# A 3x3 convolution with 2x2 max pooling: one-bank sums, two offset image lanes, and 32 steps of 12 and 20 in a written-out order

## The chip, the cores and the metric

One core of a Trainium2 chip runs the whole program. The metric is the time of one execution on the device in microseconds (us). The kernel before takes 107.98 us (median of 3 runs, 107.88 to 108.08). The engines, as the profile names them: PE (TensorE, the matmuls) with PEld (its weight loads), DVE (VectorE), ACT (ScalarE), POOL (GpSimd) and SP (SyncE, which here only issues transfers).

## The reference

```
x: (16, 64, 64, 64) f32     weight: (128, 64, 3, 3) f32     pool_size = 2
x_pad = pad(x, 1 on each side of h and w)
conv[b, co] = sum over ci, kh, kw of weight[co, ci, kh, kw] * x_pad[b, ci, kh:kh+64, kw:kw+64]
output[b, c, i, j] = max of conv[b, c, 2i:2i+2, 2j:2j+2]          # (16, 128, 32, 32)
```

## The kernel before

**Tiling.** Images go in pairs: the 64 input channels of one image lie on partitions 0 to 63 and those of the other on 64 to 127. Each matmul contracts over 64 partitions, so the two images' matmuls are issued in turn on the two halves of the array, and two run side by side. A *step* is 16 image rows (a quarter of an image) of one pair: 8 output rows, so 8 x 64 = 512 columns, one PSUM bank per image. There are 8 pairs and 32 steps.

**Two kinds of step.** Pooling needs the larger of an upper conv row y0 and a lower one y1. Let r0, r1 be the two rows of x in question and rm, rp the rows above and below; g0, g1, g2 are the kernel's rows. A *product* is three matmuls (kw = 0, 1, 2) for each image, six in all.

- A "k" step has five products. PA (two products: weights D2 = g2 - g1 on r1, G0 on rm) makes one sum; PB (two: D0 = g0 - g1 on r0, G2 on rp) makes another. After the max of both is taken, PR (G1 on the row sum r0 + r1, "ks") is added to it.
- A "w" step has four products on row sums and differences made beforehand: P2 (GM on r1 - r0, "we"), P0 (G0 on "wz"), P3 (G2 on "wy"), P1 (GP on "ws"). ACT copies minus the sum of P2 into a second bank (the seed, SE) before P0 is added to the first and P3 to the second; the max of both is taken, and then P1 is added.

After either, ACT copies the first sum to SBUF (EV/ev), DVE takes the max of the second sum and this copy, in place in PSUM (MX/mx, line 305), PE adds the last product, ACT copies the odd columns to SBUF (OD/od, line 310), DVE takes the max of even columns and these (CM/cm, line 324), and a transfer stores the result. Capitals are k steps, small letters w steps.

**Where the row operations run.** ks and ws run on DVE, wz and wy on POOL, we on DVE for the first five steps and then on POOL (all line 250). A POOL row operation is made to wait for the last DVE row operation before it in the program (`on_gpsimd`, `behind`).

**Loads.** k pairs are loaded by POOL's queue with a cast to bf16 (`kload`, line 95, tile kx), half an image pair at a time; w pairs are loaded as f32 by SP's queue, one step at a time (`wload`, line 100, two tiles wx), each issued by the store of the k step four earlier. The first two chunks of the first k pair come as f32 (kfirst, ksecond) and are cast by DVE and ACT.

**PSUM.** Four accumulators (`acc`) of two banks each, one bank per image; MX, EV, SE work on both images at once (1024 elements), OD and CM on 512.

**Order.** The program's order is written out by hand: HEAD, nine turns of STEADY, TAIL. Each token is one call; every engine runs its own instructions in this order, and waits by semaphores. One turn of STEADY has one k step and one w step, so 16 of each: 16 x 30 + 16 x 24 = 864 matmuls at line 185. Ahead of them lie 8 matmuls on ones and 28 transposes that turn the weight blocks (T*, V*).

Of the kernel before, what the change touches and what calls it, by code (L numbers as in the profile page):

```python
# [11 lines left out]
def kernel(  # L12
# [8 lines left out]

    nc = tc.nc
    FP32 = mybir.dt.float32
# [12 lines left out]
    N = NP * NQ // 2  # L48
    assert N == 16

    const = ctx.enter_context(tc.tile_pool(name="const", bufs=1))
    kx_pool = ctx.enter_context(tc.tile_pool(name="kx_pool", bufs=3))
    row_pool = ctx.enter_context(tc.tile_pool(name="row_pool", bufs=2))
    ev_pool = ctx.enter_context(tc.tile_pool(name="ev_pool", bufs=3))
    od_pool = ctx.enter_context(tc.tile_pool(name="od_pool", bufs=3))
    o_pool = ctx.enter_context(tc.tile_pool(name="o_pool", bufs=4))
# [4 lines left out]
    acc = [psum.tile([128, 2, R, W], FP32, name=f"acc_{i}") for i in range(4)]  # L61
    free = deque(range(4))
    unset = set(range(4))

# [15 lines left out]

# [7 lines left out]
    wx = [const.tile([128, H + 2, W], FP32, name=f"wx_{i}") for i in range(2)]  # L90

    def kload(j, lo, hi):
        if j not in kx:
            kx[j] = kx_pool.tile([128, H, W], BF16, name="kx")
        return nc.gpsimd.dma_start(out=kx[j][:, lo:hi, :], in_=rows_of(2 * j, lo, hi))  # L95

    def wload(i):
        j, q = divmod(i, NQ)
        lo, hi = chunk(q)
        return nc.sync.dma_start(  # L100
            out=wx[j % 2][:, lo + 1 : hi + 1, :], in_=rows_of(2 * j + 1, lo, hi)
        )
# [16 lines left out]


# [13 lines left out]
    def zero(t, h):  # L134
        return nc.tensor.matmul(
            acc[t][:, h], zeros[:, 0:128], zeros, start=True, stop=True, skip_group_check=True
        )

    turned = {}

    def turned_cols(m):
        lo, hi = BLOCKS[m] - 1, BLOCKS[m] + 3
        tp = acc[turned[m]][:, int(m == "G1")].rearrange("p a b -> p (a b)").bitcast(BF16)
        return lo, hi, tp[:, 0 : (hi - lo) * 128]

    def turn(m):
        turned[m] = turned["GM"] if m == "G1" else free.popleft()
        unset.add(turned[m])
        lo, hi, tp = turned_cols(m)
        for j in range(lo, hi):  # L150
            nc.tensor.transpose(  # L151
                tp[:, (j - lo) * 128 : (j - lo + 1) * 128],
                wq[:, j : j + 2, :].rearrange("a b c -> a (b c)"),
                ident,
            )

    def turn_out(m):
        if m != "GM":
            free.append(turned[m])
# [10 lines left out]


    def taps(t, m0, rows, start=False, skip=None, only=None):
        dst = acc[t]
        if start:
            unset.discard(t)
        for kw in (1, 0, 2):
            i0, i1 = 0, R
            if skip == 0:
                i0 = 1
            if skip == R - 1:  # L180
                i1 = R - 1
            o0, o1, c0, c1 = (0, W, 0, W) if kw == 1 else (1, W, 0, W - 1) if kw == 0 else (0, W - 1, 1, W)
            for half in range(2) if only is None else (only,):
                lo = half * CI
                nc.tensor.matmul(  # L185
                    dst[:, half, i0:i1, o0:o1],
                    wt[lo : lo + CI, m0 + kw - half, :],
                    rows(lo, i0, i1, c0, c1),
                    start=start and kw == 1,
                    stop=True,  # L190
                    skip_group_check=True,
                )

    def step1(t, q):
        first = q * R
        return lambda lo, i0, i1, c0, c1: t[lo : lo + CI, first + i0 : first + i1, c0:c1]
# [6 lines left out]
    ta, tb = {}, {}  # L203

    def pa(i):
        j, q = divmod(i, NQ)
        t = ta["k", i] = free.popleft()
        taps(t, D2, step2(kx[j], 2 * q * R + 1), start=True)
        taps(t, G0, step2(kx[j], 2 * q * R - 1), skip=0 if q == 0 else None)

    def pb(i):
        j, q = divmod(i, NQ)
        t = tb["k", i] = free.popleft()
        taps(t, D0, step2(kx[j], 2 * q * R), start=True)
        taps(t, G2, step2(kx[j], 2 * q * R + 2), skip=R - 1 if q == NQ - 1 else None)

    def pr(i):
        taps(tb["k", i], G1, step1(row["ks", i // NQ], i % NQ))

    def p2(i):  # L220
        t = ta["w", i] = free.popleft()
        taps(t, GM, step1(row["we", i // NQ], i % NQ), start=True)

    def p0(i):
        taps(ta["w", i], G0, step1(row["wz", i // NQ], i % NQ))

    def p3(i):
        taps(tb["w", i], G2, step1(row["wy", i // NQ], i % NQ))

    def p1(i, h=None):  # L230
        taps(tb["w", i], GP, step1(row["ws", i // NQ], i % NQ), only=h)

# [3 lines left out]
    def row_out(name, i):  # L236
        j, q = divmod(i, NQ)
        if (name, j) not in row:
            row[name, j] = row_pool.tile([128, HO, W], BF16, name=name)
        return row[name, j][:, q * R : (q + 1) * R, :]  # L240

    def row_in(t, first, pad):
        a = first + pad
        return t[:, a : a + 2 * R - 1 : 2, :]

    def row_op(engine, name, i, a, b, op):
        j, q = divmod(i, NQ)
        t, pad = (kx[j], 0) if name == "ks" else (wx[j % 2], 1)
        f = 2 * R * q
        return engine.tensor_tensor(  # L250
            out=row_out(name, i), in0=row_in(t, f + a, pad), in1=row_in(t, f + b, pad), op=op
        )

    def ks(i):
        inst = on_vector(row_op(nc.vector, "ks", i, 0, 1, ADD))
        if i == 0:
            behind(kload(0, *chunk(2)), inst)
# [4 lines left out]
    def we(i):  # L262
        if i < 5:
            inst = on_vector(row_op(nc.vector, "we", i, 1, 0, SUB))
            if i < 2:
                behind(wload(i + 2), inst)
        else:
            on_gpsimd(row_op(nc.gpsimd, "we", i, 1, 0, SUB))
# [4 lines left out]
    def wy(i):  # L273
        on_gpsimd(row_op(nc.gpsimd, "wy", i, 2, 0, SUB))
        j, q = divmod(i, NQ)
        if i == 0:
            kload(0, *chunk(3))
        if q == 1 and j + 1 < NP // 2:
            kload(j + 1, 0, H // 2 + 1)
        if q == 2 and j + 1 < NP // 2:  # L280
            kload(j + 1, H // 2 + 1, H)

# [3 lines left out]
    def halves(h):  # L286
        return slice(0, 2) if h is None else slice(h, h + 1)

    def evac(g, h=None):
        if g not in ev:  # L290
            ev[g] = ev_pool.tile([128, 2, R, W], FP32, name="ev")
        nc.scalar.copy(out=ev[g][:, halves(h)], in_=acc[ta[g]][:, halves(h)])  # L292
        done(g, "ev", ta, h)

    def seed(i):
        t = tb["w", i] = free.popleft()
        if t in unset:
            unset.discard(t)
            for h in range(2):
                zero(t, h)  # L300
        nc.scalar.mul(acc[t], acc[ta["w", i]], -1.0)  # L301

    def rowmax(g, h=None):
        t = acc[tb[g]][:, halves(h)]
        nc.vector.tensor_tensor(out=t, in0=t, in1=ev[g][:, halves(h)], op=MAX)  # L305

    def odd(g, h=None):
        if g not in od:
            od[g] = od_pool.tile([128, 2, R, WO], FP32, name="od")
        nc.scalar.copy(out=od[g][:, halves(h)], in_=acc[tb[g]][:, halves(h), :, 1::2])  # L310

    part = {}

    def done(g, what, tiles, h):
        part[g, what] = part.get((g, what), 0) + (2 if h is None else 1)
        if part[g, what] == 2:
            free.append(tiles.pop(g))

    def colmax(g, h=None):
        if g not in ot:  # L320
            ot[g] = o_pool.tile([128, 2, R, WO], FP32, name="o")
        s = halves(h)
        o = ot[g][:, s]
        nc.vector.tensor_tensor(  # L324
            out=o, in0=acc[tb[g]][:, s, :, 0::2], in1=od[g][:, s], op=MAX
        )
        done(g, "cm", tb, h)
        j, q = divmod(g[1], NQ)
        p = 4 * j + 2 * (g[0] == "w")
        dst = out[p : p + 2, :, q * R : (q + 1) * R, :].rearrange("b c h w -> c b (h w)")  # L330
        src = o.rearrange("p b h w -> p b (h w)")
        store = nc.scalar if h == 0 else nc.sync
        store.dma_start(out=dst[:, s], in_=src)  # L333
        if g[0] == "k" and g[1] + NQ < N and h is None:
            wload(g[1] + NQ)


    def cast_rows(first):
        inst = on_vector(
# [6 lines left out]
    def cast_more(first):  # L346
        nc.scalar.copy(out=kx[0][:, klo2 + first : khi2 : 2, :], in_=ksecond[:, first::2, :])

# [12 lines left out]
        "GP": lambda: on_vector(  # L361
            nc.vector.tensor_add(out=slots(GP), in0=gsum, in1=g1)
        ),
# [4 lines left out]
        "PA": pa, "PB": pb, "PR": pr, "P0": p0, "P1": p1, "P2": p2, "P3": p3,  # L368
        "KS": ks, "WS": ws, "E": we, "Z": wz, "Y": wy, "SE": seed,
# [85 lines left out]
```

## Time and profile before

| quantity | before |
|---|---|
| median of 3 runs | 107.98 us |
| span of the profiled execution (first to last instruction) | 106.2 us |
| mean granted PE clock | 0.982 |
| first / last matmul of line 185 starts | 5.96 / 100.5 us |
| DVE idle before line 305, waiting for PE | 11.4 us in 14 waits |
| ACT idle before line 310 / 292, waiting for PE | 11.5 us / 11.0 us |
| POOL idle before wz, waiting for DVE's ws | 24.3 us in 13 waits |
| HBM read / written | 17.07 MB / 8.39 MB |

The profile is of one execution; the span leaves out what lies around the first and last instruction. In a group of instructions "mean ns" is what one instruction's row lasts; two that follow each other may overlap, so the distance from start to start can be shorter. An issue's "us to landing" goes from the issuing instruction to the end of the last packet.

### The profile page before, as it was taken

The page shows a single profiled execution, that of the slowest core. Times are in us where ns is not written, and L with a number is a line of the kernel's source. Part 1 is how long each engine was busy: PE and PEld are TensorE (multiplying, and loading weights), DVE is VectorE, ACT ScalarE, POOL GpSimd, SP SyncE. Part 2 cuts the span into 40 slices and gives each one's busy share as a digit, 9 for nine tenths or more (in the row PEclk, how much of TensorE's full clock was granted, in tenths as well). Part 3 has the DMA queues.
Part 4 walks back from the last instruction along what each step waited for, and adds up shares of the span by engine and source line. Part 5 has one row for each costly group of instructions (what it writes and reads, how often), then busy time and mean ns, then how long its engine had stood idle before and what let it go on. Part 6 is the DMA issues. An engine that isn't in the chain of part 4 may idle for free.

```text
span 106.2 us, 2337 instructions
## 1 busy us (share of the span) xinstructions
PE 98.7 (93%) x900; PEld 51.2 (48%) x900; DVE 82.3 (78%) x115; ACT 72.3 (68%) x92; POOL 60.6 (57%) x70
## 2 busy tenths in 40 slices
PE   7879999999999999999999999999999999999800
PEld 2444445555555555555555555555555555455300
DVE  1598989889797868696977868687879688668940
ACT  4628976776867677777677676767877776775620
POOL 6208691915439494949385694949293947653000
PEclk9999999999999999999999999999999999999975
DMA  2987999999968589999968399999966503232071
GB/s 53 370 269 269 228 152 314 264 304 304 316 245 211 190 177 187 219 298 195 337 253 208 124 210 202 265 257 213 385 188 167 195 4 122 78 107 96 0 247 49
DMA packets 12619, 21.96 MB, mean 207 GB/s; under 512 B 960, under 2 KB 9280, under 8 KB 12608
## 3 DMA queue, kind: packets, MB, share of 16 engines
q1 hardware_dynamic: 11312, 18.03, 52.9%
q0 software_dynamic: 1152, 3.65, 20.1%
q8 instruction: 7, 0.11, 0.4%
q10 hardware_dynamic: 144, 0.13, 0.4%
q14 instruction: 4, 0.03, 0.2%
HBM read 17.07 MB, written 8.39 MB: 240 GB/s over the span
## 4 chain that ended last, share of the span: by engine, by line
PE 84%; DVE 6%; DMA 4%; ACT 1%; issue 1%; SPq 0%; ACTq 0%; DVEq 0%
PE acc L185 83%; DVE acc L305 5%; DMA kfirst<-in_x_dram 4%; PE acc L151 1%; DVE o L324 1%; ACT od L310 1%; DVE kx L340 0%; SPq L105 0%; ACTq L333 0%; DVEq L305 0%
## 5 line engine op out<-in xcount | busy, mean ns | idle before, releaser
L185 PEld LDWEIGHTS <-wt 64*128 64x128 bf16 x864 | 48.6, 94 | 45.1 <-issue 1.8
L305 DVE TENSOR_TENSOR acc<-acc,ev 128x1024 f32<-128x1024 f32 (+1 forms) x34 | 39.5, 1166 | 11.9 <-PE acc L185 11.4
L185 PE MATMUL acc<-kx,wt 64*128 64x504 bf16 (+3 forms) x384 | 46.6, 373 | 0.6 <-DVE kx L340 0.6
L292 ACT COPY ev<-acc 128x1024 f32<-128x1024 f32 (+1 forms) x34 | 32.6, 964 | 12.5 <-PE acc L185 11.0
L250 POOL TENSOR_TENSOR wz<-wx 128x512 bf16<-128x512 f32 x16 | 20.3, 1271 | 30.3 <-DVE ws L250 24.3
L310 ACT COPY od<-acc 128x512 f32<-128x512 f32 (+1 forms) x33 | 19.0, 574 | 12.5 <-PE acc L185 11.5
L324 DVE TENSOR_TENSOR o<-acc,od 128x512 f32<-128x512 f32 (+1 forms) x33 | 22.1, 674 | 4.5 <-ACT od L310 4.4
L250 POOL TENSOR_TENSOR wy<-wx 128x512 bf16<-128x512 f32 x16 | 20.3, 1270 | 0.0
L301 ACT ACTIVATE acc<-acc 128x1024 f32<-128x1024 f32 x16 | 16.1, 1008 | 1.0 <-PE acc L185 0.5
L250 POOL TENSOR_TENSOR we<-wx 128x512 bf16<-128x512 f32 x11 | 14.1, 1278 | 0.1
L185 PE MATMUL acc<-ws,wt 64*128 64x504 bf16 (+1 forms) x96 | 13.3, 377 | 0.4 <-DVE acc L305 0.4
L185 PE MATMUL acc<-ks,wt 64*128 64x504 bf16 (+1 forms) x96 | 13.3, 377 | 0.1
L185 PE MATMUL acc<-we,wt 64*128 64x504 bf16 (+1 forms) x96 | 13.3, 377 | 0.0
L185 PE MATMUL acc<-wz,wt 64*128 64x504 bf16 (+1 forms) x96 | 13.2, 377 | 0.0
L185 PE MATMUL acc<-wy,wt 64*128 64x504 bf16 (+1 forms) x96 | 13.2, 377 | 0.0
L250 DVE TENSOR_TENSOR ws<-wx 128x512 bf16<-128x512 f32 x16 | 10.9, 684 | 0.0
L250 DVE TENSOR_TENSOR ks<-kx 128x512 bf16<-128x512 bf16 x16 | 6.7, 417 | 0.0
L95 POOL DMA_DIRECT2D kx<-in_x_dram x8 | 4.7, 589 | 2.6 <-DVE ks L250 2.6
L403 PE MATMUL acc<-const-bfloat16-1.0 128*128 128x512 bf16 x8 | 3.2, 572 | 0.8 <-PEq L436 0.8
L250 DVE TENSOR_TENSOR we<-wx 128x512 bf16<-128x512 f32 x5 | 3.6, 722 | 0.1
L354 DVE TENSOR_TENSOR wq<-wraw 128x192 bf16<-128x192 f32 x1 | 0.5, 500 | 2.6 <-DMA wraw<-in_weight_dram 2.6
L151 PE MATMUL acc<-ident,wq 128*128 128x128 bf16 x28 | 2.1, 220 | 0.4 <-DVE wq L354 0.4
(26 smaller groups left out, 15.9 us busy)
## 6 DMA issues: line engine op xcount, KB each, us to landing
out_dram<-o SPq DMA_DIRECT2D x31, 256.0 KB, 3.8
wx<-in_x_dram SPq DMA_DIRECT2D x8, 512.0 KB, 6.8
wx<-in_x_dram SPq DMA_DIRECT2D x4, 544.0 KB, 6.0
wx<-in_x_dram SPq DMA_DIRECT2D x4, 480.0 KB, 4.8
kx<-in_x_dram POOLq DMA_DIRECT2D x3, 528.0 KB, 8.3
kx<-in_x_dram POOLq DMA_DIRECT2D x3, 496.0 KB, 8.7
kfirst<-in_x_dram SPq DMA_DIRECT2D x1, 544.0 KB, 4.3
ksecond<-in_x_dram SPq DMA_DIRECT2D x1, 512.0 KB, 4.9
```

The source lines that it names most:

```text
L95: return nc.gpsimd.dma_start(out=kx[j][:, lo:hi, :], in_=rows_of(2 * j, lo, hi))
L151: nc.tensor.transpose(tp[:, (j - lo) * 128 : (j - lo + 1) * 128], wq[:, j : j + 2, :].rearrange("a b c -> a (b c)"), ident,)
L185: nc.tensor.matmul(dst[:, half, i0:i1, o0:o1], wt[lo : lo + CI, m0 + kw - half, :], rows(lo, i0, i1, c0, c1), start=start and kw == 1, sto ...
L250: return engine.tensor_tensor(out=row_out(name, i), in0=row_in(t, f + a, pad), in1=row_in(t, f + b, pad), op=op)
L292: nc.scalar.copy(out=ev[g][:, halves(h)], in_=acc[ta[g]][:, halves(h)])
L301: nc.scalar.mul(acc[t], acc[ta["w", i]], -1.0)
L305: nc.vector.tensor_tensor(out=t, in0=t, in1=ev[g][:, halves(h)], op=MAX)
L310: nc.scalar.copy(out=od[g][:, halves(h)], in_=acc[tb[g]][:, halves(h), :, 1::2])
L324: nc.vector.tensor_tensor(out=o, in0=acc[tb[g]][:, s, :, 0::2], in1=od[g][:, s], op=MAX)
L354: on_vector(nc.vector.tensor_sub(out=slots(D2), in0=g2, in1=g1))
L403: warm = nc.tensor.matmul(acc[n // 2][:, n % 2], ones[:, 0:128], ones, start=True, stop=True, skip_group_check=True)
```

## The change

- PSUM is held as four one-bank accumulators for each of two lanes; a lane is one image of a pair. EV, MX, SE, OD and CM are done for each lane by itself: 512 elements (256 for OD and CM) instead of 1024 (512).
- The two lanes no longer go in step: a token `a+b` of the order issues the three matmuls of a product of lane 0 in turn with the three of a product of lane 1, and these may belong to different steps and products.
- 12 steps are k and 20 are w (16 and 16 before): three k pairs, five w pairs, in the sequence SEQ. So 12 x 30 + 20 x 24 = 840 matmuls. A third wx tile is added; `we` runs on DVE for 13 steps (token E) and on POOL for 7 (token e).
- Loads: the k loads have tokens of their own in the order, L0 to L5, on POOL's queue between its row operations (`kload_next`); L0 and L1 load steps 2 and 3, L2 to L5 two steps each (4-5, 6-7, 8-9, 10-11). A w load is issued behind the store of a step up to 14 places ahead of its use (LEAD), so the first store is followed by the loads of w steps 4 to 8.
- Stores: one for both lanes on SP's queue; one per lane for the last two steps.
- The order is one list of 140 products and the other engines' calls, without a repeated part.

```
+    SEQ = "KWKWKWKWWKWWKWWKWWKWWKWWKWWKWWKW"
...
-    row_pool = ctx.enter_context(tc.tile_pool(name="row_pool", bufs=2))
-    ev_pool = ctx.enter_context(tc.tile_pool(name="ev_pool", bufs=3))
-    od_pool = ctx.enter_context(tc.tile_pool(name="od_pool", bufs=3))
-    o_pool = ctx.enter_context(tc.tile_pool(name="o_pool", bufs=4))
+    row_pool = ctx.enter_context(tc.tile_pool(name="row_pool", bufs=7))
+    ev_pool = ctx.enter_context(tc.tile_pool(name="ev_pool", bufs=6))
+    od_pool = ctx.enter_context(tc.tile_pool(name="od_pool", bufs=6))
+    o_pool = ctx.enter_context(tc.tile_pool(name="o_pool", bufs=6))
...
-    acc = [psum.tile([128, 2, R, W], FP32, name=f"acc_{i}") for i in range(4)]
-    free = deque(range(4))
+    acc = [
+        [psum.tile([128, R, W], FP32, name=f"acc_{h}_{i}") for i in range(4)] for h in range(2)
+    ]
+    free = [deque(range(4)) for _ in range(2)]
...
+    wx = [const.tile([128, H + 2, W], FP32, name=f"wx_{i}") for i in range(3)]
...
+    def kload(i, n=1):
+        p, q = place["k", i]
+        lo = chunk(q)[0] if i % NQ else 0
+        hi = chunk(q + n - 1)[1]
+        nc.gpsimd.dma_start(out=ktile(i)[:, lo:hi, :], in_=rows_of(p, lo, hi))
...
+    def taps(dst, h, m0, rows, start=False, skip=None):
+        lo = h * CI
+        i0, i1 = int(skip == 0), R - int(skip == R - 1)
+        made = []
         for kw in (1, 0, 2):
...
+            made.append(
+                lambda kw=kw, o0=o0, o1=o1, c0=c0, c1=c1: nc.tensor.matmul(
+                    dst[:, i0:i1, o0:o1],
+                    wt[lo : lo + CI, m0 + kw - h, :],
+                    rows(lo, i0, i1, c0, c1),
...
+    def evac(*g):
+        ev[g] = ev_pool.tile([128, R, W], FP32, name="ev")
+        nc.scalar.copy(out=ev[g], in_=acc[g[2]][ta[g]])
+        free[g[2]].append(ta.pop(g))
+
+    def seed(i, h):
+        t = tb["w", i, h] = take(h, seeded=True)
+        nc.scalar.mul(acc[h][t], acc[h][ta["w", i, h]], -1.0)
+
+    def rowmax(*g):
+        t = acc[g[2]][tb[g]]
+        nc.vector.tensor_tensor(out=t, in0=t, in1=ev.pop(g), op=MAX)
+
+    def odd(*g):
+        od[g] = od_pool.tile([128, R, WO], FP32, name="od")
+        nc.scalar.copy(out=od[g], in_=acc[g[2]][tb[g]][:, :, 1::2])
+
+    LEAD = 14
+    held = deque(range(4, NW))
...
+        if n >= len(order_of) - 2:
+            nc.sync.dma_start(out=dst[:, h], in_=src[:, h])
+        elif stored[c, i] == 2:
+            nc.sync.dma_start(out=dst, in_=src)
+            while held and order_of.index(("w", held[0])) <= n + LEAD:
+                wload(held.popleft())
...
+    def kload_next(n):
+        if n < 2:
+            kload(n + 2)
+        else:
+            i = 2 * n
+            kload(i, min(2, NK - i))
...
+    for s in ORDER.split():
+        if s[0] == "P":
+            made = [product(n, int(i), int(h)) for n, i, h in (p.split(".") for p in s.split("+"))]
+            for matmuls in zip(*made):
+                for matmul in matmuls:
+                    matmul()
```

Some stretches of the new order (an index is the step, then the lane; S is ws):

```
g1 D0 D2 g2 TD0 GS g0 TD2 VD0 TG2 VD2 TG0 TG1 XO VG0 XE PAa.0.0+PAa.0.1 VG2 KS.0 L0 PAb.0.0+PAb.0.1
...
S.2 od.0.0 EV.1.1 P2.1.0+P2.2.1 Z.2 cm.0.0 od.0.1 MX.1.1 PBb.1.0+PBa.2.1 SE.1.0 cm.0.1 Y.2
...
CM.1.0 P1.1.0+P2.1.1 Y.4 CM.2.0 mx.2.1 PAa.3.0+PAb.3.1 SE.2.0 od.1.0 P0.2.0+PBa.3.1 L2 KS.3 EV.3.1
...
P0.3.0+P1.1.1 SE.3.1 CM.3.1 E.6 PR.3.0+P0.3.1 ev.3.0 KS.4 od.1.1 P3.3.0+P2.4.1 Z.5 od.2.0 cm.1.1
OD.3.0 cm.2.0 P2.4.0+P3.3.1 ev.3.1 mx.3.0 SE.4.1 Y.6 PAa.4.0+PAa.4.1 CM.3.0 mx.3.1 P1.3.0+PAb.4.1
...
CM.7.1 CM.7.0 Y.14 SE.12.1 P2.11.0+P0.11.1 mx.12.0 od.9.0 PAa.8.0+P0.12.1 cm.9.0 ev.11.1 L5 S.15
...
P1.11.0+P2.13.1 Z.15 ev.13.0 mx.14.1 P3.13.0+PAa.10.1 od.11.0 SE.13.1 e.15 cm.11.0 P2.14.0+P1.14.1
```

The order ends in:

```
P1.19.0+PR.11.1 mx.19.1 od.18.1 od.17.0 cm.18.1 PR.11.0+P1.19.1 OD.11.1 cm.17.0 od.19.0 CM.11.1
od.19.1 cm.19.0 OD.11.0 cm.19.1 CM.11.0
```

## The prediction

> **What bounds the kernel now.** I read the page's busy times first, then the chain of waits, then the groups by shape, then DVE's timeline, and last the transfers.
>
> ```profile
> span 106.2 us, 2337 instructions
> PE 98.7 (93%) x900; PEld 51.2 (48%) x900; DVE 82.3 (78%) x115; ACT 72.3 (68%) x92; POOL 60.6 (57%) x70
> ...
> 5.96 1.39 PE acc L185 x12
> ...
> 9.64 81.42 PE acc L185 x756
> ...
> 100.07 0.85 PE acc L185 x6
> ```
>
> The third to fifth lines are pieces of the chain (start, length, what). 756 matmuls follow each other for 81.42 us: 0.2154 us per pair, 0.646 us per product, and no other engine in between. PE bounds it. Its account: start 5.96, 432 pairs x 0.2154 = 93.05, 12 transposes after the start x 0.069 (8 take 0.55 in the chain) = 0.83, so 99.84; the last matmul ends at 100.9, so about 1.06 is lost in stalls. From there to the end of the span 5.3 us: od, cm, a store's issue on ACT's queue, od and cm of the other image, and 3.2 us from the last cm's end (103.0) on.
>
> DVE has 22% to spare, and its idle time is mostly waiting for PE. Its rows by shape, and a stretch of its timeline (start, length):
>
> ```profile
> L305 DVE TENSOR_TENSOR acc<-acc,ev 128x1024 f32<-128x1024 f32 x30 | 36.8, 1228 | 11.7 <-PE acc L185 11.4 <-ACT ev L292 0.2
> L324 DVE TENSOR_TENSOR o<-acc,od 128x512 f32<-128x512 f32 x31 | 21.2, 690 | 3.5 <-ACT od L310 3.5
> L305 DVE TENSOR_TENSOR acc<-acc,ev 128x512 f32<-128x512 f32 x4 | 2.7, 696 | 0.2
> L324 DVE TENSOR_TENSOR o<-acc,od 128x256 f32<-128x256 f32 x2 | 0.8, 424 | 1.0 <-ACT od L310 0.8
> ...
> 22.82 0.69 DVE L324 TENSOR_TENSOR o<-acc,od 128x512 f32<-128x512 f32 x1
> 23.42 0.68 DVE L250 TENSOR_TENSOR we<-wx 128x512 bf16<-128x512 f32 x1
> 24.02 0.42 DVE L250 TENSOR_TENSOR ks<-kx 128x512 bf16<-128x512 bf16 x1
> 24.36 0.68 DVE L250 TENSOR_TENSOR ws<-wx 128x512 bf16<-128x512 f32 x1
> ```
>
> A row of 0.69 is followed after 0.60: back to back, an instruction costs about 0.085 less than its row.
>
> **Change 1, fewer matmuls.** 840 instead of 864: 12 pairs x 0.2154 = 2.59 us less, on the bounding engine. Against it: in before, the products at an image's upper and lower edge leave out one of eight rows in both images at once (64 of 512 columns, 3 x 64 columns a product; by the pair's 0.2154 for 512 columns 0.08 us), 8 times, 0.64 us, which the mean 0.2154 holds. In the new order only two of six such products (step 0 and step 7) stand beside their twin; elsewhere the partner has full length. About 0.46 us goes back. The rest of the pairing I cost at nothing: in before too the two matmuls of a pair have different weights, rows and banks.
>
> **Change 2, head and tail.** PAa.0 still needs kfirst and its cast, so the start stays at 5.96; 8 transposes come after it instead of 12: 0.55. Behind the last product there are now OD, CM of 256 elements: 1.27 us (od 0.41, then OD 0.26 later, then CM 0.42, hand-overs 0.04 each) instead of 2.1 with a store's issue in between, then the same 3.2: 4.4 instead of 5.3.
>
> Without stalls: 5.96 + 90.47 + 0.46 + 0.55 + 4.4 = 101.8 us of span. The old span is reached at 4.4 us of stalls; so the stalls decide.
>
> **Change 3, DVE and ACT in half-size pieces.** DVE back to back: MX 64 x 0.61 = 39.0; CM 64 x 0.34 (0.424 - 0.085) = 21.8; ks 12 x 0.335 = 4.0; ws 20 and we 13 x 0.605 = 20.0; weights and casts at the head 4.4; together 89 us, against 91 us of PE work. MX's 0.61 is one of three gaps between 512-element MX in the tail (starts at 97.18, 97.91, 98.52, 99.31: 0.73, 0.61, 0.79). Bounds: 0.61 and their mean 0.71, 6.4 us more over 64; I take 0.61, the gap of every row that waits for nothing, and keep the other. In a sentence of its own: the Trainium skill (Perfetto Trace Analysis, Optimizing Scalar/DVE Operations) gives DVE about 125 ns of overhead on PSUM and 60 on SBUF and advises larger operations where the engine is saturated; here CM, which reads PSUM, shows 0.605 - 512/0.96 GHz = 0.07 us, and by the page's figure an estimate of DVE's sum would be 6 us more.
>
> ACT back to back: the two 512-element ev of step 15 take 1.07 together, so 0.48 each; EV and SE 104 x 0.48, OD 64 x 0.26, head 4: 71 us. POOL: 47 row operations x 1.225 (start to start), six issues x 0.58, head 3: 64 us. Neither bounds.
>
> By place: of DVE's 89 us, 40.7 stand ahead of the 60th of 140 products. DVE starts at 3.7 (weights landed), so done at 44.4 at best; PE gets there at 6.5 (start and transposes) + 59 x 0.646 = 44.6. DVE is full for the first 60 products; between products 34 and 59 it has 16.9 us to do in 16.2. I charge 0.8 us of stall (0.7 of excess, 0.1 of hand-overs); up to 2.6 if MX costs 0.71 (26 of them ahead of the 60th product).
>
> **Change 4, the k loads at their new places.** These rows (all of before's kx loads have 7.5 to 8.8 us) stand against it:
>
> ```profile
> kx<-in_x_dram POOLq DMA_DIRECT2D x3, 528.0 KB, 8.3
> kx<-in_x_dram POOLq DMA_DIRECT2D x3, 496.0 KB, 8.7
> wx<-in_x_dram SPq DMA_DIRECT2D x1, 544.0 KB, 9.5
> ```
>
> The third is the w load issued at 14.6. Before, the k loads had some 15 us: steps 0 to 3 hold 108 pairs, so step 4 begins at about 30.5, and its load was issued at 15.7 (its own row: 8.6).
>
> *L2* (steps 4, 5) stands behind Z.2, Y.2, e.3, Z.3, Y.4 on POOL, and Z.2 behind S.2 on DVE. wload(2) follows E.0 (8.7) and lands 7.0 later (its row in before), so E.2 runs from 15.7, S.2 is done at 16.9; five operations of 1.225 bring L2 to 23.1, and 8.6 more to 31.7. KS.4 needs it, and on DVE cm.1.1, cm.2.0 and mx.3.0 are queued behind KS.4; mx.3.0 must be done for product 38 (P1.3.0) at 6.5 + 37 x 0.646 = 30.4. KS.4 and the three take 1.7, so KS.4 is due at 28.7: **3.0 us late**, on DVE and PE alike. Bounds: 2.0 if PE is already a microsecond late there; 5.8 if Y.4 waits for its rows (wload(4) behind the first store at 15.1, landing 9.5 later, 24.6), which the five w loads in a row could do.
>
> *L5* (steps 10, 11) stands behind Z.14, e.13, Y.14, these behind KS.7, this behind MX.7.0, which waits for product 81 (6.5 + 81 x 0.646 = 58.8, and 0.2 for its last matmul's end). MX 0.61, KS 0.42, three POOL operations 3.7: L5 at 63.9; with the 7.5 to 7.8 of the rows from 60 us on it lands at 71.6. PAa.10.1 is product 99, due at 69.8: **1.7 us late** (1.6 to 2.9 by the longest row). L0, L1, L3, L4 have 7.5 to 16 us and cost nothing; L0 (5.6 to 13.1 for product 11 at 13.0) is even.
>
> In a sentence of its own: the Trainium skill (DMA: Bandwidth & Descriptors, Anatomy of one DMA) gives a load by this path 2.0 us plus its bytes at 436 GB/s, for these 1.08 MB read an estimate of 4.5 us, by which both loads would be in time; the rows here show 7.5 to 8.8 and do not bear it out.
>
> **Sum.** 101.8 + 0.8 + 3.0 + 1.7 = 107.3 us of span. The profiled execution's span of 106.2 lies 1.8 under the median of its runs (107.98); with the same 1.8: **109.1 us**, 1.1 slower than before.
>
> **Rivals.**
> - *The loads land in time*, because POOL reaches them earlier or a load takes the 4.4 to 4.9 us of the quietest rows (wx at 2.7, ksecond at 4.2). For it: the DMA engines' share is 0.71 in the stretch from 30 to 40 us, against 0.96 to 1.04 from 10 to 30. Against it: eight rows of 7.5 and more, at 60 us too. Stalls 0.8 plus some 0.3: 101.8 + 1.1 + 1.8 = **104.7**, faster. It decides from where both loads together are less than 3.6 late instead of 4.7, about half a microsecond each: near. The Trainium skill's DMA page, named above, speaks for this one.
> - *DVE loses its overlap*: with 64 MX and 64 CM each waiting for a result just made, each costs its row and starts after the former one's end: 64 x 0.696 + 64 x 0.424 + ks 5.0 + ws 13.7 + we 9.4 + head 4.6 = 104.3; from 3.7, with 0.5 idle and 3.2 at the end 111.7, so **113.5**. Half of it, 103.9 of span from DVE alone, is under what the loads give, so it decides from six tenths on. Against it: in before, an MX, with PE's sum and ACT's copy to wait for, still started 0.61 after the CM ahead of it (59.45 to 60.06).
> - *The five w loads in a row* hold Y.4 back: L2's upper bound, 2.8 more, **111.9**.
> - *Pairs of unlike products don't run side by side*: then each such product takes twice 0.646, some 60 us more; nothing in the rows speaks for it.
>
> **How the numbers follow.** Forecast 0.52, loads in time 0.26, DVE without overlap 0.14, w loads 0.07, unpaired 0.01. The likeliest gives 109.1, its own range is 106.6 to 111.5 (L2 2.0 to 5.0, L5 1.0 to 2.9, DVE 0.4 to 1.6), which reaches under 107.8: of its 0.52, 0.06 is faster and 0.05 the same. A measurement of this kernel tells some 0.2% (0.2 us) from no change. Faster: 0.26 + 0.06 + 0.01 of the DVE case = 0.33; same 0.06; slower 0.61. The range for 8 in 10 reaches to the loads in time below and the w loads above: 104.6 to 112.2.
>
> **What would show it.** PE's rows with a gap of 1.5 us or more ahead of product 38 and of product 99, the releaser DVE's mx behind KS.4, and the kx load; DVE idle at KS.4 until a transfer; six kx issues of 7.5 us or more; MX of 512 elements 0.61 apart where DVE is full; line 185 with 840 matmuls at 0.108 each between stalls; 4.4 us from the last matmul to the end. It is wrong if PE runs through 23 to 35 us and 60 to 75 us without a gap: then a load took under 6 us or POOL came to it earlier, and the time is under 106.

## The result and the profile after

| quantity | before | after |
|---|---|---|
| median of the runs | 108.03 us (run again beside it) | 116.38 us (114.80, 116.10, 116.66, 119.89) |
| ratio to before, with 95% interval | | 1.0675 [1.0578, 1.0773]: slower |
| profiled execution, span | 106.2 us | 114.80 us, 113.0 us |
| mean granted PE clock | 0.982 | 0.975 |
| first matmul of the products starts | 5.96 us | 6.03 us |
| end of the last matmul to end of span | 5.3 us | 5.3 us |

The ratios here and below leave disturbed executions out, so that a ratio can lie below the quotient of the medians, and none is given where too few are left.

The page of after, its first lines, the granted clock in 40 slices of 2.8 us, and the groups that answer to DVE's lines shown of before:

```profile
span 113.0 us, 2473 instructions
PE 100.8 (89%) x877; PEld 53.1 (47%) x877; DVE 93.1 (82%) x184; ACT 81.4 (72%) x177; POOL 64.6 (57%) x74
...
PEclk9999999999998599999999999999999999999995
...
L300 DVE TENSOR_TENSOR acc<-acc,ev 128x512 f32<-128x512 f32 x64 | 42.3, 691 | 4.1 <-PE acc L211 2.4
...
L315 DVE TENSOR_TENSOR o<-acc,od 128x256 f32<-128x256 f32 x64 | 24.9, 416 | 3.2 <-ACT od L304 2.5
...
kx<-in_x_dram POOLq DMA_DIRECT2D x2, 528.0 KB, 9.1
kx<-in_x_dram POOLq DMA_DIRECT2D x2, 496.0 KB, 8.3
```

PE is busy in 89% of the span instead of 93%, and no other engine is full. The slices 13 and 14 have a low clock; before had no such place ahead of its last matmul. DVE's rows have the sizes that were forecast (0.69 and 0.42 us), and the two-step k loads take 7.8 to 9.4 us (each of the two lines gives the middle of two loads).

The chain of waits, whole where PE runs and broken where it does not (start, length, what):

```profile
35.73 32.71 PE acc L211 x280
...
72.25 7.81 DMA kx<-in_x_dram
...
80.11 25.37 PE acc L211 x232
```

The stretch around the larger break, in the timeline of all engines (start, length; in brackets the idle time before and what ended it):

```profile
34.59 0.42 DVE L260 TENSOR_TENSOR ks<-kx 128x512 bf16<-128x512 bf16 x1 [3.46 <-DMA kx<-in_x_dram]
...
34.93 0.75 DVE L315 TENSOR_TENSOR o<-acc,od 128x256 f32<-128x256 f32 x2
...
35.60 0.69 DVE L300 TENSOR_TENSOR acc<-acc,ev 128x512 f32<-128x512 f32 x1
35.73 1.46 PE L211 MATMUL acc<-kx,wt 64*128 64x512 bf16 x6 [3.06 <-DVE o L315]
...
36.97 0.63 PE L211 MATMUL acc<-ws,wt 64*128 64x512 bf16 x1
```

KS.4 stands still for 3.46 us until L2 has landed; behind it on DVE come the two cm and mx.3.0, and PE is idle for 3.06 us. It goes on with product 37 (products are counted from 1, as in the prediction), as soon as the second cm has freed a bank; the prediction had named product 38 and mx.3.0. What was not forecast is in the last line: a matmul now lasts 0.63 us instead of 0.38. The table by stretches has the clock (columns: stretch, its length, busy us and instructions of PE, PEld, DVE, ACT, POOL, then granted clock, DMA share, GB/s):

```profile
34.00:36.00 2.00, 0.27 (x2) 0.22 (x4) 1.41 (x4) 0.56 (x1) 0.91 (x1) 0.92 0.29 112
36.00:38.00 2.00, 2.00 (x12) 0.90 (x10) 2.00 (x4) 0.61 (x2) 2.00 (x3) 0.50 0.93 281
38.00:40.00 2.00, 2.00 (x17) 1.29 (x14) 1.76 (x4) 1.35 (x4) 0.68 (x2) 0.73 0.95 190
```

From 35.7 to 39.1 us the granted clock is 0.50; 3.41 us at half speed cost a full PE 1.7 us. The wait is thus paid for half again after it is over. The four executions of after lie in the order of their mean granted clock: 0.975 with 114.80 us, 0.968 with 116.10, 0.963 with 116.66, 0.945 with 119.89. An estimate from these means (the missing share of the clock, times two, times the span) puts 5.7, 7.3, 8.5 and 13.0 us at half speed. The other three spans are 1.3, 1.9 and 5.1 us longer than the profiled one, and by the estimate lost clock makes up 0.8, 1.4 and 3.7 us of that. At which places they lost it, no trace shows.

The account of after's span, by the starts of its 840 matmuls (839 distances, 0.1077 each without a stall):

| term | us | forecast |
|---|---|---|
| first matmul starts | 6.03 | 5.96 |
| 839 x 0.1077, and the last matmul's row of 0.38 | 90.74 | 90.47 |
| losses up to 20 us (head) | 2.85 | 0.55 |
| gap ahead of product 37 (L2) | 3.42 | 3.0 |
| half clock behind it | 1.7 | not in the sum |
| gap ahead of product 99 (L5) | 1.81 | 1.7 |
| all other losses (edges, DVE) | 1.2 | 1.26 |
| last matmul's end to the end | 5.30 | 4.4 |
| span | 113.0 | 107.3 |

The row "other" is what is left of 10.96 us of losses in all. The 1.7 is worked out from the clock (half of 3.41 us). Before has 1.61 us of losses, about 1.1 of them up to 20 us.

### The profile page after: what moved, and what is told of

Same layout as the page of the kernel before. It is cut to its first block, busy times and chain, and to the rows that moved or that the text cites. A ratio compares the mean times of both kernels' runs of the same rounds, so it can differ in the third digit from the quotient of the medians.

```text
span 113.0 us, 2473 instructions
## 1 busy us (share of the span) xinstructions
PE 100.8 (89%) x877; PEld 53.1 (47%) x877; DVE 93.1 (82%) x184; ACT 81.4 (72%) x177; POOL 64.6 (57%) x74
## 4 chain that ended last, share of the span: by engine, by line
PE 51%; DMA 7%; POOL 3%; DVE 3%; issue 1%; DVEq 0%; POOLq 0%
PE acc L211 51%; DMA kx<-in_x_dram 7%; DVE o L315 2%; POOL wz L260 1%; POOL we L260 1%; POOL wy L260 1%; DVE acc L300 1%; DVEq L483 0%; POOLq L260 0%; DVEq L300 0%
## 5 line engine op out<-in xcount | busy, mean ns | idle before, releaser
L300 DVE TENSOR_TENSOR acc<-acc,ev 128x512 f32<-128x512 f32 x64 | 42.3, 691 | 4.1 <-PE acc L211 2.4
L291 ACT COPY ev<-acc 128x512 f32<-128x512 f32 x64 | 36.0, 593 | 6.3 <-PE acc L211 5.5
L211 PE MATMUL acc<-ws,wt 64*128 64x504 bf16 (+1 forms) x120 | 31.6, 383 | 0.0
L211 PE MATMUL acc<-wy,wt 64*128 64x504 bf16 (+1 forms) x120 | 30.7, 377 | 0.0
L296 ACT ACTIVATE acc<-acc 128x512 f32<-128x512 f32 x40 | 23.1, 585 | 9.7 <-DVE o L315 4.9
L211 PE MATMUL acc<-wz,wt 64*128 64x504 bf16 (+1 forms) x120 | 29.4, 385 | 0.0
L211 PE MATMUL acc<-we,wt 64*128 64x504 bf16 (+1 forms) x120 | 28.3, 377 | 0.2 <-DVE we L260 0.2
L315 DVE TENSOR_TENSOR o<-acc,od 128x256 f32<-128x256 f32 x64 | 24.9, 416 | 3.2 <-ACT od L304 2.5
L304 ACT COPY od<-acc 128x256 f32<-128x256 f32 x64 | 22.3, 379 | 6.2 <-PE acc L211 5.7
L211 PE MATMUL acc<-ks,wt 64*128 64x504 bf16 (+1 forms) x72 | 16.9, 377 | 0.0
L260 DVE TENSOR_TENSOR we<-wx 128x512 bf16<-128x512 f32 x13 | 8.8, 682 | 0.3 <-DMA wx<-in_x_dram 0.3
```

What stands on the lines that cost most here:

```text
L211: lambda kw=kw, o0=o0, o1=o1, c0=c0, c1=c1: nc.tensor.matmul(dst[:, i0:i1, o0:o1], wt[lo : lo + CI, m0 + kw - h, :], rows(lo, i0, i1, c0, c1),
L260: return engine.tensor_tensor(out=r, in0=t[:, f + a : f + a + 2 * R - 1 : 2, :], in1=t[:, f + b : f + b + 2 * R - 1 : 2, :], op=op,)
L291: nc.scalar.copy(out=ev[g], in_=acc[g[2]][ta[g]])
L296: nc.scalar.mul(acc[h][t], acc[h][ta["w", i, h]], -1.0)
L300: nc.vector.tensor_tensor(out=t, in0=t, in1=ev.pop(g), op=MAX)
L304: nc.scalar.copy(out=od[g], in_=acc[g[2]][tb[g]][:, :, 1::2])
```

## The experiments

Two theories stood at the start. **The gaps**: the time is lost where two k loads come too late, and in what PE does after such a gap. **Half-size DVE work** (a rival): DVE cannot keep up in 64 + 64 small pieces, and then moving the loads brings nothing. A third, *the five w loads in a row*, blames the transfers that compete with L2.

**Loads earlier.** e1 moves L2, e2 moves L5, e3 both; nothing else changes.

L2, in e1 and e3:

```
-        P0.0.0+P0.0.1 OD.0.1 S.1 P3.0.0+P3.0.1 Z.1 CM.0.1 ev.0.1 ev.0.0 mx.0.1 PAa.2.0+PAa.2.1 OD.0.0 Y.1
+        P0.0.0+P0.0.1 OD.0.1 S.1 P3.0.0+P3.0.1 Z.1 CM.0.1 ev.0.1 ev.0.0 mx.0.1 PAa.2.0+PAa.2.1 OD.0.0 Y.1 L2
...
-        CM.1.0 P1.1.0+P2.1.1 Y.4 CM.2.0 mx.2.1 PAa.3.0+PAb.3.1 SE.2.0 od.1.0 P0.2.0+PBa.3.1 L2 KS.3 EV.3.1
+        CM.1.0 P1.1.0+P2.1.1 Y.4 CM.2.0 mx.2.1 PAa.3.0+PAb.3.1 SE.2.0 od.1.0 P0.2.0+PBa.3.1 KS.3 EV.3.1
```

L5, in e2 and e3:

```
-        SE.9.1 e.14 P0.10.0+P1.8.1 MX.6.1 P3.10.0+P0.9.1 od.8.1 MX.6.0 ev.10.0 Y.12 P1.8.0+PR.6.1 ev.9.1
+        SE.9.1 e.14 P0.10.0+P1.8.1 MX.6.1 P3.10.0+P0.9.1 od.8.1 MX.6.0 ev.10.0 Y.12 L5 P1.8.0+PR.6.1 ev.9.1
...
-        CM.7.1 CM.7.0 Y.14 SE.12.1 P2.11.0+P0.11.1 mx.12.0 od.9.0 PAa.8.0+P0.12.1 cm.9.0 ev.11.1 L5 S.15
+        CM.7.1 CM.7.0 Y.14 SE.12.1 P2.11.0+P0.11.1 mx.12.0 od.9.0 PAa.8.0+P0.12.1 cm.9.0 ev.11.1 S.15
```

> Only L2, the load of k steps 4 and 5, is moved ahead: from behind Y.4 to behind Y.1 on POOL's queue, so it is issued at about 17.3 us instead of 25.1. Theory 'late loads': it lands by about 26 us, KS.4 no longer waits, the 3.4 us gap of PE at 32 to 36 us goes, and with it the 1.7 us that the half clock behind it costs: span 113.0 - 5.0 = about 108.0, time about 109.8; the gap at product 99 stays. Rival 'DVE is full': the wait was only where DVE's backlog showed, and PE loses 2 us or more of the 5.0 again in smaller stalls between 30 and 70 us: span 110 or more.

> Only L5, the load of k steps 10 and 11, is moved ahead: from behind Y.14 to behind Y.12 on POOL's queue, issued some 11 us earlier. Theory 'late loads': the 1.8 us gap of PE ahead of product 99 goes, the gap at 32 to 36 us and the half clock stay: span about 111.2, time about 113. Rival 'DVE is full': less than 1 us.

> Both loads, L2 and L5, are moved ahead as in the two runs with one. Theory 'late loads': the gains add, 5.0 + 1.8: span about 106.2, time about 108.0, which is before's. Rival 'DVE is full': under half of it, span 109.5 or more.

| kernel | median us | ratio to before [95%] | span | losses |
|---|---|---|---|---|
| e1 | 111.28 | 1.0161 [1.0080, 1.0241] | 110.0 | 7.12 |
| e2 | 113.73 | none given | 112.4 | 9.82 |
| e3 | 109.58 | 1.0107 [1.0065, 1.0148] | 107.7 | 4.78 |

In e1, L2 is issued at 17.48 instead of 25.14 and lands sooner too (in the microsecond of its issue the share of the transfers on SP's queue is 34% of the DMA engines' time, in after 101%); the page's clock line has no low slice left:

```profile
PEclk9999999999999999999999999999999999999997
```

L2's row in its transfer view:

```profile
kx<-in_x_dram POOLq DMA_DIRECT2D x1, 528.0 KB, 6.3
```

That time varies: 6.3 to 8.8 us in the five kernels with L2 at this place (e1, e3, e5, e6, e7), 9.1 to 10.2 in the five with L2 at after's place (after, e2, e4, e10, e11). The 3.4 us gap is gone and the half clock with it. In its place a loss of 0.89 at 29 us has come: Y.4 now waits for step 4's w rows, whose load runs beside the earlier L2. The gap ahead of product 99 stays (1.91). In e2 it is the other way round: product 99 runs through, and the gap of 4.18 at 36 us and its half clock stay in the profiled execution. (The fastest of e2's four executions, 111.49 us, has a mean clock of 0.993, which leaves 1.5 us at half speed: less than one piece of 3.41, so that there the half clock did not come.) e3 has neither gap. So both loads are causes, each at its own place, and together with the half clock they make up most of the slowdown (1.0675 to 1.0107). The rival falls for this part, but e3 is still slower than before, by 1%.

**The half clock apart from the wait.** e4 lets PE run 13 matmuls on zeros, into a bank that the next product clears, where it would stand idle; e10 is the same with L5 early (to be compared with e2).

```
+        if s == "PAa.4.0+PAa.4.1":
+            for _ in range(13):
+                nc.tensor.matmul(
+                    acc[1][free[1][0]], zeros[:, 0:128], zeros, start=True, stop=True,
+                    skip_group_check=True,
+                )
```

> The loads stay where the change has them. 13 matmuls on zeros are put ahead of product 37, into the free bank that this product clears and fills next, so PE is busy through most of the wait for KS.4. Theory 'the idle gap brings the half clock': the wait stays at 3 to 3.5 us of line 211's matmuls, but the granted clock stays 1.0 between 35 and 40 us, and 1.7 us come back: span about 111.3. Rival 'the half clock is not from the gap': span 113.0 and the clock falls all the same.

> L5 early, and 13 matmuls on zeros ahead of product 37 as in the run that filled the gap. To be compared with L5 early alone (113.7), where the clock fell behind the gap at 32 to 36 us. Theory 'an idle gap of 3 us brings the half clock': with the gap filled and the second gap gone the clock stays full to the end of the matmuls: about 112.0. Rival 'the half clock comes anyway, once in a run': it falls somewhere else, and the time stays at 113 to 114.

e4: 115.79 us, 1.0645 [1.0587, 1.0702], not told apart from after. Its stretches say why (columns as before):

```profile
36.00:38.00 2.00, 1.85 (x19) 0.73 (x17) 2.00 (x5) 1.42 (x3) 1.92 (x3) 1.00 1.10 308
...
77.00:80.00 3.00, 0.70 (x7) 0.21 (x6) 0.88 (x2) 0.90 (x3) 2.18 (x2) 1.00 0.62 196
80.00:84.00 4.00, 4.00 (x24) 1.52 (x22) 2.05 (x4) 1.74 (x5) 2.00 (x2) 0.57 0.02 6
```

The wait for L2 is as long as ever (3.39), but the clock behind it is 1.00, so that it is idleness and not the late load that halves the clock. PE then comes to product 99 1.2 us earlier; L5 is issued earlier by as much (71.05), but takes 8.5 us instead of 7.8, PE idles 2.30 us there instead of 1.64, and now the half clock falls behind this gap, from 80.1 to 83.5 us, for a loss of 1.71. In e10, which has no second gap, the trace shows the gain: the clock is full to the last matmul while the wait for L2 is still 3.20, and the span is 110.4 beside e2's 112.4. Of these 2.0 us the half clock is 1.7. The rest nearly cancels: e10 starts 0.8 earlier and waits 1.0 less for L2, and loses 1.0 more in the head and 0.5 elsewhere. The times, 112.11 us, 1.0329 [1.0277, 1.0380], against e2's median of 113.73, don't show it by themselves, since e2's one execution without the half clock (111.49) is level with e10's.

**The same place, smaller loads.** e8 leaves L2 and L5 where they are and loads one step at a time.

```
-            kload(i, min(2, NK - i))
+            if n in (2, 5):
+                kload(i)
+                kload(i + 1)
+            else:
+                kload(i, 2)
```

> On the changed kernel as it was, the loads stay at their places, but L2 and L5 each become two loads, one step each, in a row. Theory 'a k load is late by its size': the first half lands after some 6 us (the one-step loads of the head took 4.9 to 7.1) instead of 9.4 and 7.8, so the wait for KS.4 falls from 3.4 to under 1, the one ahead of product 99 to under 0.5; time 116.4 - 4 or more, if the half clock goes with the gap: about 111 to 112. Rival 'a k load has a fixed latency of 8 us whatever its size': no change, 115 to 116.

111.47 us, 1.0287 [1.0214, 1.0361], span 109.5. The first halves, in the two transfer views:

```profile
kx<-in_x_dram POOLq DMA_DIRECT2D x1, 272.0 KB, 7.9
...
kx<-in_x_dram POOLq DMA_DIRECT2D x1, 256.0 KB, 6.9
```

Half the bytes land only 1.5 and 0.9 us sooner (9.4 and 7.8 in after): beside the other queues a transfer's time is mostly not its own bytes. The gaps fall by about as much, 3.42 to 1.97 and 1.81 to 0.89 (not to under 1 and 0.5, as was expected), and the PE idle time of 1.61 brings no half clock; so 2.4 us of gap and 1.7 us of half clock are saved, and the ratio falls by 4 points. In the profiled execution the head, too, loses 1.0 less than in after.

**The five w loads.** e11 shortens the lead of the w loads, so that fewer compete with L2.

```
-    LEAD = 14
+    LEAD = 10
```

> LEAD 10 instead of 14, nothing else: the first store is followed by two w loads and not by five. Rival of the prediction 'the five w loads hold the k load back': L2 lands some 1 us or more earlier than after 9.4, the wait for KS.4 falls by as much. Theory 'L2 is late by its place and its size': L2 still takes 8.3 or more, the gap stays over 2.5 us, the time within 1 us of the changed kernel's 115 to 116.

124.18 us, 1.1464 [1.1418, 1.1510]. L2 still takes 9.8 us (issued 25.57), with a gap of 3.87, so the five in a row are not the cause. Competition as such is not ruled out: here too two w loads are issued just ahead of L2 (24.83 and 25.36). And the later w loads are now late; the waits show where (total us, times, longest):

```profile
POOL we L260 <- DMA wx<-in_x_dram: 13.2, 2, 8.9
```

PE loses 6.09 us at 74 us, released by E.12 on DVE, whose ws ahead of it had waited 4.3 us for w rows too, and 2.97 at 90. Idle times of 3.51, 5.85 and 2.81 us were each followed by the half clock, for 3.41, 6.83 and 3.41 us.

**What is left in e3: DVE beside POOL.** In e3 E.4 and Y.4, a row operation on DVE and one on POOL, overlap, and the DVE one lasts 1.75 us:

```profile
25.21 1.45 POOL L260 TENSOR_TENSOR wy<-wx 128x512 bf16<-128x512 f32 x1 [1.80 <-DMA wx<-in_x_dram]
25.45 1.75 DVE L260 TENSOR_TENSOR we<-wx 128x512 bf16<-128x512 f32 x1
...
28.19 0.39 PE L211 MATMUL acc<-we,wt 64*128 64x512 bf16 x1 [0.70 <-DVE o L315]
```

e7 is e3 with Y.4 behind E.4. e5 is e3 with two edits at the head: ksecond issued without waiting for D2, and Y.0 behind Z.0, so that GP on DVE has no POOL operation beside it.

Against e3, e7:

```
-        CM.1.0 P1.1.0+P2.1.1 Y.4 CM.2.0 mx.2.1 PAa.3.0+PAb.3.1 SE.2.0 od.1.0 P0.2.0+PBa.3.1 KS.3 EV.3.1
-        S.3 PAb.3.0+PBb.3.1 ev.2.0 E.4 P3.2.0+P1.2.1 SE.1.1 Y.3 MX.3.1 PBa.3.0+P0.1.1 od.2.1 cm.1.0 mx.2.0
+        CM.1.0 P1.1.0+P2.1.1 CM.2.0 mx.2.1 PAa.3.0+PAb.3.1 SE.2.0 od.1.0 P0.2.0+PBa.3.1 KS.3 EV.3.1
+        S.3 PAb.3.0+PBb.3.1 ev.2.0 E.4 Y.4 P3.2.0+P1.2.1 SE.1.1 Y.3 MX.3.1 PBa.3.0+P0.1.1 od.2.1 cm.1.0 mx.2.0
```

Against e3, e5:

```
-        "D2": lambda: load_second(
-            on_vector(nc.vector.tensor_sub(out=slots(D2), in0=g2, in1=g1))
-        ),
+        "D2": lambda: on_vector(nc.vector.tensor_sub(out=slots(D2), in0=g2, in1=g1)),
...
-        GM VG1 Y.0 PBa.0.0+PBa.0.1 EV.0.0 GP TGM EV.0.1 PBb.0.0+PBb.0.1 VGM E.0 TGP Z.0 MX.0.1 P2.0.0+P2.0.1
+        GM VG1 PBa.0.0+PBa.0.1 EV.0.0 GP TGM EV.0.1 PBb.0.0+PBb.0.1 VGM E.0 TGP Z.0 Y.0 MX.0.1 P2.0.0+P2.0.1
...
+            load_second(warm)
```

> On the version with both loads early, Y.4 on POOL is put behind E.4 on DVE, where it was ahead of KS.3; Y.4 there waited for its rows and then ran beside E.4, which took 1.75 us instead of 0.68. Theory 'a DVE row operation stands still while POOL's runs': E.4 is back at 0.7, the stall of 0.9 us at 28 us goes, time about 108.8. Rival 'the stall is DVE's backlog there': E.4 gets shorter, PE's stall stays above 0.6.

> On the version with both loads early, the head is changed: ksecond is issued behind the warm matmul at 3 us and no longer behind D2, and Y.0 goes behind Z.0 on POOL, so that GP on DVE does not run beside it. Theory 'the head is bound by ksecond's landing (10.4 to 10.9) and by GP, stretched from 0.5 to 1.5 us beside Y.0': ksecond lands by 9 us, GP takes 0.5, the stalls of PE up to 20 us fall from 1.6 to under 0.8: 0.8 to 1.2 us less than the 109.6, about 108.6. Rival 'the transfers share one bandwidth, so an earlier ksecond delays kfirst': the first matmul comes later by as much, no gain.

The two DVE operations in e7 and in e5:

```profile
26.46 0.69 DVE L260 TENSOR_TENSOR we<-wx 128x512 bf16<-128x512 f32 x1 [0.30 <-DMA wx<-in_x_dram]
```

```profile
7.56 0.49 DVE L359 TENSOR_TENSOR wq<-gsum,wraw 128x192 bf16<-128x192 f32 x1
```

Both fall to their plain size (E.4 1.75 to 0.69; GP 1.47 in e3, 1.51 in after, to 0.49), so the standing still is real. Neither time falls. In e7 (110.54 us, 1.0166 [1.0070, 1.0261]) the stall at 28 us is gone, as the theory had it, but the collision has only moved: POOL now stands still for 3.19 us ahead of Y.4 and is 1.1 us later with Z.4, KS.4 on DVE runs beside Z.4 and takes 1.50 us instead of 0.42, and PE loses 0.97 at product 37, released by a cm behind KS.4. In e5 (109.65 us, 1.0118 [1.0030, 1.0207]) ksecond lands at 8.83 instead of 10.40, but e3 had no wait for it that could be won: its first matmul came late, at 6.92. E.1 now waits 0.87 us for its wx rows and PE loses 0.33 at product 11, which the earlier ksecond may have caused by taking its share of the transfers; no run shows that. Moving a wait is not removing it.

**The tail.** e6 is e3 with the stores of lane 1 of the last two steps on ACT's queue.

```
-            nc.sync.dma_start(out=dst[:, h], in_=src[:, h])
+            (nc.scalar if h == 1 else nc.sync).dma_start(out=dst[:, h], in_=src[:, h])
```

> On the version with both loads early, the last four half stores alternate between SP's and ACT's queue (lane 1 on ACT). Theory 'the last store waits for three issues of 0.45 us on SP': 5.3 us from the last matmul's end to the end of the span become 4.6, time about 108.9. Rival 'the landing of the last store sets the end, whatever the queue': no change, 109.6.

109.21 us, 1.0089 [1.0051, 1.0128], not told apart from e3's 1.0107. From the last matmul's end to the end 5.16 us instead of 5.31: ACT's store waits for its cm, and OD is queued behind it on ACT, so that the last CM ends 1.75 us after the last matmul (104.21) instead of 1.20 (103.63 in e3), which uses up most of what the stores gained.

**Can it be mended?** e9 takes after, loads step 4's rows behind e.3 (token L6) and step 5's behind Y.4 (L7) (so that neither the w rows of step 4 nor KS.4 wait), L5 ahead of Y.11, and the last step's lane-1 store on ACT's queue. e12 has e9's load places, Y.0 behind Z.0, and stores both lanes of the last steps in one transfer.

Both, against after:

```
+        elif n >= 6:
+            kload(n - 2)
...
-        PBb.2.0+PBb.2.1 MX.1.0 SE.2.1 P0.1.0+PR.1.1 MX.2.1 PR.1.0+P0.2.1 MX.2.0 OD.1.1 e.3 ev.1.0
+        PBb.2.0+PBb.2.1 MX.1.0 SE.2.1 P0.1.0+PR.1.1 MX.2.1 PR.1.0+P0.2.1 MX.2.0 OD.1.1 e.3 L6 ev.1.0
...
-        CM.1.0 P1.1.0+P2.1.1 Y.4 CM.2.0 mx.2.1 PAa.3.0+PAb.3.1 SE.2.0 od.1.0 P0.2.0+PBa.3.1 L2 KS.3 EV.3.1
+        CM.1.0 P1.1.0+P2.1.1 Y.4 CM.2.0 mx.2.1 PAa.3.0+PAb.3.1 SE.2.0 od.1.0 P0.2.0+PBa.3.1 L7 KS.3 EV.3.1
...
-        PBa.6.0+P2.9.1 od.7.1 S.11 ev.8.0 P3.8.0+PBa.6.1 Y.11 mx.8.1 SE.10.0 cm.7.1 PBb.6.0+PBb.6.1 mx.8.0
+        PBa.6.0+P2.9.1 od.7.1 S.11 ev.8.0 P3.8.0+PBa.6.1 L5 Y.11 mx.8.1 SE.10.0 cm.7.1 PBb.6.0+PBb.6.1 mx.8.0
...
-        CM.7.1 CM.7.0 Y.14 SE.12.1 P2.11.0+P0.11.1 mx.12.0 od.9.0 PAa.8.0+P0.12.1 cm.9.0 ev.11.1 L5 S.15
+        CM.7.1 CM.7.0 Y.14 SE.12.1 P2.11.0+P0.11.1 mx.12.0 od.9.0 PAa.8.0+P0.12.1 cm.9.0 ev.11.1 S.15
```

The stores of e9:

```
-            nc.sync.dma_start(out=dst[:, h], in_=src[:, h])
+            (nc.scalar if (c, h) == ("w", 1) else nc.sync).dma_start(out=dst[:, h], in_=src[:, h])
```

The stores of e12 (its Y.0 as in e5):

```
-        if n >= len(order_of) - 2:
+        if n >= len(order_of):
```

> Three edits on the changed kernel. L2 becomes two loads: step 4 behind e.3 on POOL (about 22.5 us), step 5 behind Y.4; so it does not compete with the load of w step 4 at 17.7 us. L5 goes ahead of Y.11, where POOL waits for PE anyway. The last store of w step 19's lane 1 goes on ACT's queue. Theory: the wait for KS.4 falls under 0.5 us without the collision of Y.4 and E.4, no gap ahead of product 99, no half clock: losses of 3.5 us against 4.8 with both loads early, 0.4 us less at the end: span 106, time about 107.8, the same as before. Rival 'DVE is full': no better than 109.3.

> The version with step 4's load split off and L5 ahead of Y.11, with two more edits: Y.0 behind Z.0 on POOL, so GP on DVE runs alone; and the last two steps store both lanes in one transfer, so SP issues four stores at the end instead of six (none on ACT). Theory 'SP's issues delay the last store by 0.7 us and GP's stretch costs 0.2': from the last matmul's end to the end 4.6 us instead of 5.2, the first stalls 0.2 us less: time 107.4, faster than before's 108.3. Rival 'the last 256 KB land as late as four halves, and the head is bound by its transfers': 108.2, no change.

e9: 108.24 us, 0.9991 [0.9965, 1.0017]; e12: 108.28 us, 1.0011 [0.9984, 1.0039]. Both are level with before; no version was faster than before. Two lines of e9's page:

```profile
PE 99.4 (93%) x877; PEld 53.7 (50%) x877; DVE 93.9 (88%) x184; ACT 81.3 (76%) x177; POOL 65.1 (61%) x75
...
PEclk9999999999999999999999999999999999999995
```

PE is at 93% again and the clock has no low place. Where the 24 matmuls have gone: e9's span 106.57 against before's 106.18 is 24 x 0.1077 = 2.58 less of matmuls, losses of 3.74 instead of 1.61 (2.13 more: the head 0.4, the stretch from 20 to 50 us 1.6, where DVE was forecast to be full), a first matmul at 6.93 instead of 5.96 (0.97 more), and 0.12 less at the end; together 0.4 more. The tail of e12 is 4.65, by 0.65 below after's, as it should be if the issues one after another delay the end; its head loses 2.40 where e9's loses 1.57, its first matmul comes 0.66 earlier, and its span of 106.3 is 0.3 below e9's; the medians do not tell the two apart. What these mends leave is above all the head. After's first matmul comes at 6.03; over the thirteen kernels from after on, whose work up to there is nearly the same, it lies between 5.72 and 7.08, 0.5 to 1.2 us behind the landing of kfirst. An early start does not last: those that start early mostly lose more up to 20 us, and first matmul and head losses together make 8.1 to 9.4 us (8.9 in after, 8.5 in e9, 8.7 in e12), against 7.1 in before. No run takes this back.

## Why the prediction was right or wrong

**Direction and places: right.** Slower was forecast, with both gaps, the loads behind them and the queue behind KS.4 (only the last link was another: a cm and product 37). L2's gap was 3.42 for 3.0, L5's 1.81 for 1.7. e1 and e2 take one away each and leave the other. That L2's size came so near is in part luck. It landed 2.9 us later than forecast: it was issued at 25.14 instead of 23.1, since S.2 was done at 18.8 instead of 16.9 (its w rows had landed by 14.6, so it was DVE and PE that were late, from the head on), and it took 9.4 instead of 8.6. PE, held up in the same head, came to product 37 2.5 us later than forecast, and the two errors nearly cancel. The estimate of 4.5 us for such a load, by the figure of the Trainium skill (DMA: Bandwidth & Descriptors, Anatomy of one DMA), is not borne out: these loads took 9.4 and 7.8 us, and 6.3 in e1.

**Pacing and pairing: right.** 0.1077 us a matmul outside the stalls, for unlike products too; CM and MX as sized (where DVE has no wait, the next instruction starts 0.60 us behind an MX and 0.33 behind a CM). Edges and DVE came to 1.2 us for 1.26, but that is luck: the same terms come to 1.8 in e4, where the clock is full from 34 to 40 us, and to 2.2 in e9 and e12, which have no large gap under which DVE's lateness could lie hidden. "DVE loses its overlap" did not come: 840 matmuls end at 107.7, and DVE's idle ahead of MX is 4.1 us in all.

**The step that failed in its mechanism: a stall was priced at its own length.** The step "3.0 us late, on DVE and PE alike" went into the sum as 3.0. What followed was a clock of 0.50 for 3.41 us, 1.7 us more, for which the sum had no term; e10 takes it off without moving L2, and in e4 it moves behind the other gap. The wait was right, its price short by 1.7 us. The range had the same flaw: its upper end had longer waits in it but nothing that a wait brings after it. It took more than this step, though, to leave the range: without the 1.7 the profiled 114.8 us would still be 113.1, above 112.2, and only without the head's 2.3 (next) as well does it come to 110.8. The median lies another 1.6 us above the profiled execution; the executions there have a lower mean clock, but the cause stays open.

**The head, a mis-sized term, and the largest.** "So the start stays at 5.96; 8 transposes come after it instead of 12: 0.55" held for the start and not for what follows: 2.85 us. The timeline of after there:

```profile
7.40 1.26 POOL L260 TENSOR_TENSOR wy<-wx 128x512 bf16<-128x512 f32 x1 [1.30 <-DVE wq L359]
7.51 1.51 DVE L361 TENSOR_TENSOR wq<-gsum,wraw 128x192 bf16<-128x192 f32 x1
...
10.89 1.14 ACT L340 CAST kx<-ksecond 128x512 bf16<-128x512 f32 x2 [1.85 <-DMA ksecond<-in_x_dram]
...
11.56 1.02 PE L211 MATMUL acc<-kx,wt 64*128 64x512 bf16 x7 [1.05 <-ACT kx L340]
```

ksecond took 6.3 us (4.9 before) beside L0 and the w loads that are now issued next to it, its cast waits 1.85 us and PE loses 1.23 at product 6: I had counted the transposes and not what the head's transfers share. Next to that, the two groups of transposes cost 0.44 and 0.69 (the second with a wait of 0.19 for E.0 on DVE) instead of 0.55 together, and one matmul on zeros (line 153, ahead of product 8), which before does not have and the sum left out, costs 0.44. GP lasts 1.51 beside POOL's Y.0, but that decides nothing here: in e10, where GP takes 0.50, PE loses as much ahead of product 6 (1.38).

**The tail, a mis-sized term.** The last CM ends 1.2 us after the last matmul, as forecast (1.27). Then "the same 3.2" was 4.1: the last two steps issue four stores one after another on one queue, 1.96 us, behind two stores of other steps. The last result is done at 108.9 and its store is issued at 109.75; in before the last result was done at 103.04 and its store issued at 103.06.

```profile
108.20 1.96 SPq L325 DMA_DIRECT2D out_dram<-o  x4
```

**Sum.** 107.3 forecast + head 2.3 + half clock 1.7 + L2 0.4 + L5 0.1 + tail 0.9 + start and the last row 0.3 = 113.0. With the forecast's 1.8 around the span that is 114.8, the profiled execution's time.

## What to carry to other kernels

Price a load that is moved behind other work by the landing rows of the busiest stretch, and then follow the queue behind whoever waits for it; that step named both places. Then ask what a gap of PE leaves behind: here gaps of 2.3 to 3.8 us cost 1.7 us more each time the half clock followed. And price a kernel's head by what its transfers share, not by its instructions alone. And where DVE is 88% busy and the loads have no slack, 2.6 us of saved matmuls are easily given back: e9 and e12 have no large stall left and still only equal before.

## What the runs showed of the hardware

- **The clock after a gap.** PE idle for 2.30, 2.81, 3.06, 3.51, 3.82 and 5.85 us was followed by a granted clock of 0.5 for 3.41 us (6.83 after the longest); idle for 1.61, 1.64 and 1.74 us was not. In all these traces the clock changes in steps of 3.41 us: every piece between two changes is a whole multiple (30.72 us is nine, 71.68 is 21). So it matters how a gap lies on the steps. In e2 the step that ended at 34.05 us held the first 1.89 us of the gap and was not followed by the half clock; the next, with the last 1.93 us, was, from 37.47 on, 1.5 us after PE had gone on. The Trainium skill (TensorE: Matmul & The Clock Gate, HAM oscillation — how this bites in real kernels) has gaps over about 3.4 us as those to avoid; here 2.30 was enough.
- **DVE stands still beside POOL.** DVE operations with both inputs in SBUF wait for a POOL row operation that started before them: GP 1.51 instead of 0.49, E.4 1.75 instead of 0.69, KS.4 in e7 1.50 instead of 0.42. Where DVE starts first, POOL waits: in e10 E.0 started 0.03 us ahead of Y.0 and kept 0.69, and Y.0 took 1.78 instead of 1.26. The Trainium skill (SBUF — State Buffer, SBUF: two separate sides) says that the two share an exclusive lock and that the loser blocks fully; these rows agree. MX and CM, with one input in PSUM, kept their size: in after 54 MX beside POOL and 10 without it both average 0.690 us.
- **Halving a load hardly halves its time** where the queues are full: 528 KB 9.4 us, 272 KB 7.9; in e9 and e12 another 272 KB took 8.2 and 7.3.
- **Left open:** why kfirst lands up to 1.4 us apart (5.15 to 6.58) between kernels with the same start; why most executions of after have a lower mean clock than the profiled one.
